# Strassen's scheme in the last group of each down projection, with the embedding's projection recorded inside it

## The chip, the cores and the metric

The kernel runs on one core of a Trainium2 chip. A core has a matrix engine (TensorE, PE in the profile, with PEld for its weight loads), a vector engine (VectorE, DVE), an activation engine (ScalarE, ACT), a general engine (GpSimd, POOL) and a queue that issues DMAs (SyncE, SP). The engines run side by side, each in its own order, and wait for one another through semaphores. Operands lie in SBUF; matmuls write to banks of PSUM. The metric is the device time of one execution in microseconds.

## What is computed

The reference is a decoder trunk of two layers over 512 tokens of width 1024, in float32. The first layer mixes tokens with two kinds of attention (latent and sliding-window), the second with forgetting attention. What follows the attention is the same in both:

```python
x = _layer_norm(DN_ALPHA * x + m, ln1_g[i], ln1_b[i])
x = _layer_norm(DN_ALPHA * x + _sq_relu_mlp(x, w_up[i], w_down[i]), ln2_g[i], ln2_b[i])
gate = jax.nn.sigmoid(x @ ple_w_gate[i] + ple_b_gate[i])
x = x + gate * (p[i] @ ple_w_proj[i])

def _sq_relu_mlp(x, w_up, w_down):
    return jnp.square(jax.nn.relu(x @ w_up)) @ w_down
```

Here m is the attention's output, w_up is 1024 x 4096, w_down 4096 x 1024, ple_w_proj 256 x 1024 (the projection of the per-layer embedding p) and ple_w_gate 1024 x 1024.

## The kernel before, in words

**Products.** Each float32 factor is split into a rounded part (hi) and the rest (lo), and a product is made of three matmuls, hi hi, hi lo and lo hi (`mm3`). So each matmul of 128 x 128 by 128 x 512 comes in threes. ACT makes the rounded part; the rest is a subtraction on DVE or POOL (`split`, `piece`, `tt` at line 488).

**The feed-forward part.** The 32 blocks of 128 hidden features are worked in 8 groups of four. `up` makes one block (24 matmuls, then relu and square on ACT). A group's share of the down projection is added to x. For groups 0 to 6 this is `down_pairs`, Strassen's scheme in Winograd's form: the 512 tokens are taken as two halves, the 1024 output columns as two halves, and the four feature blocks as two pairs, and 7 products of sums and differences take the place of 8. `forms` makes the sums of activations of a pair (A11, A12, A22, S1 to S4), each with its hi and lo. `form` makes those of the weights (11, 21, 22, T1 to T4) from four raw blocks. PRODUCTS names for each product the activation form, the PSUM bank (A, B or C, two of each, one per token block) and the quarter of the output that it is added to. The banks go on accumulating from product to product, and after each product DVE adds the bank to that quarter of x (line 1350). For the last group, `down` makes the plain product: for each of the four token blocks and each half of the columns, four feature blocks are accumulated in one bank and added to x by `add_sum`, which also gives the row sums. After each token block comes `after`, which is the second layer norm (`layer_norm`) and the transposition of the block (`to_X`).

**Behind it.** `ple_proj` loads the embedding, splits it and multiplies it with two weight pieces (8 banks of 6 matmuls, lines 1370 and on). `ple` and `gate` then multiply the normed x with the gate's eight weight pieces, 24 matmuls per token block and half, and combine.

**Weights.** `weight_pieces` lists all weights in the order of their use, in pieces of 128 x 1024, which lie in that order in DRAM. `weights` hands them out and records the loads and splits ahead of use, up to 12 of the 12 buffers "w". A piece takes two of them, a form of the scheme one. Raw data comes through 2 buffers "raw" for pieces and 6 buffers "t5" for the scheme. Activations, forms, rows and partial results share 42 buffers "u".

**Order.** Nothing is issued directly: every operation is recorded with an engine, an assumed duration and the buffers that it reads and writes. `Plan.schedule` then orders the operations of all engines by a greedy simulation: on each engine, the operation goes first whose priority (its place in the record, plus `shift`) is least among those that are ready. Buffers of one kind are given in the order of the record. A flag `port` marks operations of DVE that the plan lets run only while no operation of POOL runs, and the other way around. In the attention parts the shifts are written out (EVEN, ODD). On the chip each engine keeps the order so found.

Of the kernel before, what the change touches and what calls it, by code (L numbers as in the profile page):

```python
# [36 lines left out]
P = 128  # L37
S = 512
D = 1024
TB = 4  # L40
# [20 lines left out]
WARM = 8  # L61
SPLIT = "ddddppdpppdppdpdpppp"
SCRATCH = {"e": 8 * 32 * 384, "c": 16 * S, "x": S * D}

# [29 lines left out]
def weight_pieces():  # L94
# [8 lines left out]
    def tail(l):  # L103
        def up(js):
            for j in js:
                add(D, lambda I, j=j: _cols(I["w_up"][l], slice(j * P, j * P + P)))
        up(range(4))
        for g in range(8):
            up(range(4 * g + 4, 4 * g + 6) if g < 7 else ())
            for j in range(4):  # L110
                add(D, lambda I, fb=4 * g + j: _rows(I["w_down"][l], [fb], slice(0, D)), "s" if g < 7 else "w")
            up(range(4 * g + 6, 4 * g + 8) if g < 7 else ())
        for h in range(2):
            add(D, lambda I, h=h: _rows(I["ple_w_proj"][l], (0, 1), slice(512 * h, 512 * h + 512)))
        for h in range(2):
            for q in range(4):
                add(D, lambda I, h=h, q=q: _rows(I["ple_w_gate"][l], (2 * q, 2 * q + 1), slice(512 * h, 512 * h + 512)))
# [314 lines left out]
class Trunk:  # L432
    LOOK = 5

    def __init__(self, plan, A, out, scratch, pieces):
        self.p, self.nc, self.A, self.out = plan, plan.nc, A, out
        self.scratch = scratch
        self.dram = {k: Buf(None, None, None, k) for k in scratch}
        self.pieces, off = [], 0
        for w, _, _ in pieces:  # L440
            self.pieces.append((off, w))
            off += P * w

        self.items, i = [], 0
        while i < len(pieces):
            if pieces[i][2] == "s":
                self.items += [(f, i, p) for f in self.FORMS for p in range(2)]
                i += 4
            else:
                self.items.append(("w", i, 0))  # L450
                i += 1
        self.wi, self.wt, self.ahead, self.raws = 0, [], 0, {}
        self.turn = 0
        self.X = plan.buf("xh", (P, KD, S), R, "xh"), plan.buf("xl", (P, KD, S), R, "xl")
        self.ident = plan.buf("ident", (P, P), F, "ident")
        self.op = plan.op
# [100 lines left out]

    FORMS = ("11", "21", "T2", "T1", "T3", "22", "T4")
    FORM_POOL = {"T3", "T4", "l21", "lT1", "l22"}

    def form(self, f, i, p):
# [8 lines left out]
        def less(key, out, x, y, r, w):  # L570
            self.tt(512, key in self.FORM_POOL, out, x, y, ALU.subtract, r, w)
        if f == "T2":
            t3 = self.raws[p][2] = self.u("T3")
            less("T3", lambda: t3[:], lambda: b[:, h[1]], lambda: a[:, h[1]], [(a, 1), (b, 1)], [t3])
            less("T1", lambda: a[:, h[1]], lambda: a[:, h[1]], lambda: a[:, h[0]], [(a, 0)], [(a, 1)])
            less("T2", lambda: a[:, h[0]], lambda: b[:, h[1]], lambda: a[:, h[1]], [(a, 1), (b, 1)], [(a, 0)])
# [50 lines left out]
    def rsqrt(self, y, v, r, w, n=1, scale=0):  # L627

        t, hv = self.small("nt", n), self.small("nh", n)
        d = lambda fn, rr, ww, dur=0.07: self.dve(1, fn, rr, ww, dur=dur)  # L630
        d(lambda e: e.tensor_scalar(y().bitcast(I32), v().bitcast(I32), 1, None, ALU.arith_shift_right), r, [w])
# [205 lines left out]
    def e_bias(self):  # L837
# [12 lines left out]
        self.nsinks = self.p.buf("sm16", (P, 8), F, "nsinks")  # L850
        self.dve(8, lambda e: e.tensor_scalar(self.nsinks[:], self.sinks[:], -1.0, None, ALU.mult), [self.sinks], [self.nsinks])

# [362 lines left out]
    def layer_norm(self, x, st, g, b):  # L1215

        nm, q, v, y = (self.small(n, 4) for n in ("nm", "sq", "va", "rs"))
        c = lambda z: z[:, 0:1]
        d = lambda fn, r, w, dur=0.07: self.dve(1, fn, r, w, dur=dur)
        d(lambda e: e.tensor_scalar(c(nm), st[:, 0:1], st[:, 1:2], -1.0 / D, ALU.add, ALU.mult), [st], [nm], 0.1)  # L1220
# [44 lines left out]

    def ffn(self, x, after):

        rt = self.up_first()
        for g in range(7):
            rl = [self.up() for _ in range(2)]  # L1270
            self.down_pairs(g, rt, x)
            rl += [self.up() for _ in range(2)]
            rt = [self.forms(*rl[j:j + 2]) for j in (0, 2)] if g < 6 else rl
        self.down(rt, x, after)

# [53 lines left out]

    def down_pairs(self, g, rt, x):  # L1330

        banks, seen = {}, set()
        for f, k, (th, h) in self.PRODUCTS:
            ws = [self.weights() for _ in rt]
            for i in range(2):
# [11 lines left out]
                if g == 0 and (tb, h) not in seen:  # L1347
                    self.dve(S, lambda e, b=b, xx=xx: e.scalar_tensor_tensor(xx[:], xx[:], ALPHA, b[:], ALU.mult, ALU.add), [b], [xx])
                else:
                    self.dve(S, lambda e, b=b, xx=xx: e.tensor_tensor(xx[:], xx[:], b[:], ALU.add), [b], [xx])  # L1350
                seen.add((tb, h))

    def down(self, rl, x, after):

        rt = [self.p.buf("t5", (P, 2, 512), R, "r") for _ in rl]
        for a, r in zip(rl, rt):
            self.split(S, lambda a=a: a[:], lambda r=r: r[:, 0, :], lambda r=r: r[:, 1, :], [a], [r], psum=False)
        ws = [self.weights() for _ in range(4)]
        for tb in range(TB):
            ts, st = slice(tb * P, (tb + 1) * P), self.small("st", 4)  # L1360
            for h in range(2):
                cs = slice(512 * h, 512 * (h + 1))
                b = self.bank()
                for j in range(4):
                    r, w = rt[j], ws[j]
                    self.mm3(512, lambda b=b: b[:], (lambda r=r, ts=ts: r[:, 0, ts], lambda r=r, ts=ts: r[:, 1, ts]),
                             (lambda w=w, cs=cs: w[0][:, cs], lambda w=w, cs=cs: w[1][:, cs]), j == 0, j == 3,
                             [r] + list(w), [b])
                self.add_sum(x[tb][h], b, st, h)
            after(tb, st)  # L1370

    def ple_proj(self, l):

        ph, pl = ([self.u(n, R) for _ in range(2)] for n in ("ph", "pl"))
        for k in range(2):
            raw = self.load("u", (P, S), lambda k=k: self.A["pT"][l, k], "praw")
            self.split(S, lambda raw=raw: raw[:], lambda k=k: ph[k][:], lambda k=k: pl[k][:], [raw], [ph[k], pl[k]], psum=False)
        out = {}
        for h in range(2):
            w = self.weights()  # L1380
            for tb in range(TB):
                ts = slice(tb * P, (tb + 1) * P)
                b = self.bank()
                for k in range(2):
# [3 lines left out]
                             [ph[k], pl[k]] + list(w), [b])  # L1388
                pr = self.u("pr")
                self.act(S, lambda e, b=b, pr=pr: e.mul(pr[:], b[:], 0.5), [b], [pr], True)  # L1390
                out[h, tb] = pr
        return out

# [26 lines left out]
    def run(self):  # L1420
        A = self.A
        for l in range(2):
# [24 lines left out]

            self.ffn(x, ln2)
            pr = self.ple_proj(l)
            bg = self.row(8 + l, "bg")  # L1450
# [43 lines left out]
```

## Time and profile before

| | |
|---|---|
| median of 3 runs | 1263.97 us (1263.49 to 1265.16) |
| the profiled execution | 1265.41 us, of which the span of the profile is 1263.6 |
| clock granted to TensorE, mean | 0.995 |
| DMA | 132.83 MB, 105 GB/s in the mean |

The stages of the profile, in us from the start of the span: attention of layer 0 to about 200, its feed-forward part to about 555, the gate to about 612; attention of layer 1 to about 884, its feed-forward part to about 1203, the gate to the end at 1263.6. In the profile a row names line, engine, operation, and the tiles written and read by their names in the program, without the buffer numbers. A matmul's duration includes the time in which it overlaps the next one; the rate is read from start to start, or from the length of a stretch that is full. The busy time of a DVE operation includes time in which it was held off from SBUF.

### The profile page before, as it was taken

How to read it: one execution, taken by the hardware profiler on the slowest of the kernel's cores; microseconds unless marked ns; L12 is line 12 of the kernel's file. 1: busy time of each engine (PE TensorE's matmuls, PEld its weight loads, DVE VectorE, ACT ScalarE, POOL GpSimd, SP SyncE). 2: the span in 40 equal slices, each digit the busy share in tenths (PEclk: the TensorE clock that was granted, in tenths of full speed). 3: DMA queues.
4: the chain of work that ended last, by engine and by line, in shares of the span. 5: the costliest groups of instructions: out<-in, count | busy, mean ns of one | idle time of the engine just before them, and what ended most of it. 6: DMA issues, size and time to landing. Idle time of an engine off the chain costs nothing.

```text
span 1263.6 us, 17349 instructions
## 1 busy us (share of the span) xinstructions
PE 1233.4 (98%) x6108; PEld 1042.6 (83%) x6108; DVE 949.7 (75%) x1695; ACT 687.2 (54%) x1352; POOL 505.2 (40%) x408
## 2 busy tenths in 40 slices
PE   8988999999999999999999999899999999999998
PEld 6987888988888887888897888788888888888887
DVE  5568877899888887585543587868899878897564
ACT  5658874645444445353444697945654554445451
POOL 2545432444445444312213466331544545443120
PEclk9999999999999999999999999999999999999999
DMA  5422432233223422423232422352223332332131
GB/s 197 141 88 85 145 122 85 83 101 123 89 89 100 133 75 76 154 65 131 91 104 93 147 70 92 134 183 68 84 84 114 120 100 84 117 117 82 68 117 50
DMA packets 46791, 132.83 MB, mean 105 GB/s; under 512 B 5984, under 2 KB 8672, under 8 KB 46704
## 3 DMA queue, kind: packets, MB, share of 16 engines
q1 hardware_dynamic: 46704, 131.72, 31.6%
q8 instruction: 48, 0.79, 0.3%
q14 instruction: 39, 0.32, 0.1%
HBM read 126.03 MB, written 4.62 MB: 103 GB/s over the span
## 4 chain that ended last, share of the span: by engine, by line
PE 81%; ACT 8%; DVE 6%; issue 2%; DMA 2%; POOL 1%; SPq 0%; ACTq 0%; DVEq 0%; POOLq 0%
PE mm L512 31%; PE s L512 21%; PE t L512 16%; PE o L512 10%; ACT t L664 2%; PE t L523 2%; ACT wh L551 1%; DVE wl L488 1%; DMA raw<-in_wall_dram 1%; ACT pth L502 1%; DVE qlo L753 1%; ACT q L755 1%; ACT q L752 1%; DVE t L659 1%; POOL wl L488 0%
## 5 line engine op out<-in xcount | busy, mean ns | idle before, releaser
L488 POOL TENSOR_TENSOR wl<-raw,wh 128x1024 fp32r<-128x1024 f32 (+4 forms) x78 | 182.4, 2340 | 405.5 <-ACT wh L551 376.4
L551 ACT CAST wh<-raw 128x1024 fp32r<-128x1024 f32 (+5 forms) x150 | 152.2, 1018 | 148.0 <-DMA raw<-in_wall_dram 73.7
L488 POOL TENSOR_TENSOR wf<-raw,wf 128x512 fp32r<-128x512 f32 x84 | 122.1, 1475 | 173.4 <-ACT wf L584 156.8
L512 PE MATMUL mm<-xh,wh 128*128 128x512 f32 (+1 forms) x416 | 161.7, 389 | 2.8 <-DVE k L766 0.8
L512 PE MATMUL mm<-xl,wh 128*128 128x512 f32 (+1 forms) x416 | 159.6, 384 | 0.2 <-DVE xl L503 0.2
L512 PE MATMUL mm<-xh,wl 128*128 128x512 f32 (+1 forms) x416 | 159.7, 384 | 0.0
L488 DVE TENSOR_TENSOR wl<-raw,wh 128x1024 fp32r<-128x1024 f32 (+4 forms) x72 | 102.5, 1423 | 47.8 <-ACT wh L551 38.3
L584 ACT CAST wf<-raw 128x512 fp32r<-128x512 f32 x168 | 100.9, 615 | 34.9 <-PE t L512 15.3
L512 PE MATMUL t<-wf,rh 128*128 128x512 f32 x336 | 103.8, 390 | 0.7 <-DVE x L1350 0.7
L673 POOL TENSOR_SCALAR t<-t,st 128x256 f32<-128x256 f32 (+3 forms) x128 | 69.3, 561 | 79.3 <-DVE st L670 61.4
L512 PEld LDWEIGHTS mm<-xh,wh 128*128 128x128 f32 x416 | 78.8, 189 | 19.7 <-ACT q L755 2.2
L512 PEld LDWEIGHTS mm<-xh,wl 128*128 128x128 f32 x416 | 78.7, 189 | 15.8 <-DVE wl L503 0.4
L512 PEld LDWEIGHTS mm<-xl,wh 128*128 128x128 f32 x416 | 78.7, 189 | 14.4 <-DVE xl L503 0.5
L488 DVE TENSOR_TENSOR wf<-raw,wf 128x512 fp32r<-128x512 f32 x84 | 77.4, 936 | 17.4 <-ACT wf L584 17.1
L512 PE MATMUL mm<-wh,xh 128*128 128x384 f32 (+5 forms) x232 | 82.8, 357 | 5.9 <-DVE qlo L753 2.8
L512 PE MATMUL mm<-wl,xh 128*128 128x384 f32 (+5 forms) x232 | 80.6, 348 | 0.2 <-POOL wl L488 0.2
L512 PE MATMUL mm<-wh,xl 128*128 128x384 f32 (+5 forms) x232 | 80.7, 348 | 0.0
L1350 DVE TENSOR_TENSOR x<-x,t 128x512 f32<-128x512 f32 x100 | 67.0, 679 | 12.3 <-PE t L512 10.3
L664 ACT ACTIVATE t<-t,st 128x256 f32<-128x256 f32 (+3 forms) x128 | 68.7, 540 | 12.7 <-DVE st L659 10.6
L512 PEld LDWEIGHTS t<-wf,rh 128*128 128x128 f32 x336 | 62.8, 188 | 14.7 <-DVE x L1350 1.8
L512 PE MATMUL s<-wf,rh 128*128 128x512 f32 x224 | 69.0, 389 | 0.0
L512 PE MATMUL t<-wf,rl 128*128 128x512 f32 x168 | 65.4, 389 | 0.0
(296 smaller groups left out, 3273.9 us busy)
## 6 DMA issues: line engine op xcount, KB each, us to landing
raw<-in_wall_dram SPq DMA_DIRECT2D x183, 512.0 KB, 3.5
ck<-scratch_c SPq DMA_DIRECT2D x16, 256.0 KB, 3.8
raw<-in_wall_dram SPq DMA_DIRECT2D x9, 384.0 KB, 3.3
x<-in_xT_dram SPq DMA_DIRECT2D x8, 256.0 KB, 5.3
x<-in_xn_dram SPq DMA_DIRECT2D x8, 256.0 KB, 5.3
g<-in_rows_dram SPq DMA_DIRECT2D x8, 256.0 KB, 5.1
b<-in_rows_dram SPq DMA_DIRECT2D x8, 256.0 KB, 5.3
scratch_x<-x SPq DMA_DIRECT2D x8, 256.0 KB, 2.0
```

The source lines that it names most:

```text
L488: fn = lambda e: e.tensor_tensor(out(), a(), b(), op)
L502: self.act(n, lambda e: e.copy(hi(), src()), r, w, psum)
L512: return [self.nc.tensor.matmul(o(), a(), b(), start=s, stop=e, **kw) for o, a, b, s, e in prods]
L523: lambda: [self.nc.tensor.transpose(o(), i(), self.ident[:]) for o, i in items],
L551: self.act(w, lambda e: e.copy(hi[:, :w], raw[:, :w]), [raw], [hi])
L584: self.act(512, lambda e: e.copy(t[:, h[0]], src()), [key], [(t, 0)])
L659: return e.tensor_tensor_reduce(t[:, offs[i] + a:offs[i] + z], b[:, c + a:c + z], ad(), -scale, init, ALU.add, ALU.min, nm[:, i:i + 1])
L664: self.act(n, lambda e, i=i, tt=tt: e.activation(tt(), tt(), AF.Exp, bias=nm[:, i:i + 1], scale=-1.0, accum_out=sm[:, i:i + 1]), [(nm, i)] ...
L673: self.pool(0.13 + 1.21e-3 * n, lambda e, i=i, tt=tt: e.tensor_scalar(tt(), tt(), rc[:, i:i + 1], 1.0, ALU.mult, ALU.mult), [rc], [(t, i)])
L752: self.act(S, lambda e, q2=q2, rs=rs: e.copy(q2[rs, :], bank[rs, :]), [bank], [(q2, 0)], True)
L753: self.dve(S, lambda e, q2=q2, lo=lo, rs=rs: e.tensor_tensor(lo[rs, :], bank[rs, :], q2[rs, :].bitcast(F), ALU.subtract), [bank, (q2, 0)], ...
L1350: self.dve(S, lambda e, b=b, xx=xx: e.tensor_tensor(xx[:], xx[:], b[:], ALU.add), [b], [xx])
```

## The change

1. The last group goes through `form`, `forms` and `down_pairs` like the others; `down` is removed. `down_pairs` gets two functions, `after` and `between`, for the last group alone.
2. In the last group the products are in another order (LAST): S1 before S2 and S4 before S3. So the upper half of the tokens (blocks 0 and 1) is complete after the fifth product, and the lower half (blocks 2 and 3) after the seventh. The last addition to a quarter of x is `add_sum`, and when both halves of a block are done, `after` is recorded. The last two products have their priority moved ahead by 200 places. The weight forms T1 and T2 are made in the other order there.
3. `ple_proj` is taken apart. Its loads, splits and two weight pieces are recorded before the last group (`ple_load`), its matmuls after the third product, with a priority 400 places later and the banks "o" and "s". The two pieces stand ahead of the last four down pieces in `weight_pieces`.
4. The small DVE operations of `rsqrt`, `layer_norm` and the sinks get the flag `port`.

```diff
+AHEAD = 200
+LATER = 400
...
             up(range(4 * g + 4, 4 * g + 6) if g < 7 else ())
+            for h in range(2 if g == 7 else 0):
+                add(D, lambda I, h=h: _rows(I["ple_w_proj"][l], (0, 1), slice(512 * h, 512 * h + 512)))
             for j in range(4):
-                add(D, lambda I, fb=4 * g + j: _rows(I["w_down"][l], [fb], slice(0, D)), "s" if g < 7 else "w")
+                add(D, lambda I, fb=4 * g + j: _rows(I["w_down"][l], [fb], slice(0, D)), "s" if g < 7 else "t")
...
-    FORMS = ("11", "21", "T2", "T1", "T3", "22", "T4")
+    FORMS = {"s": ("11", "21", "T2", "T1", "T3", "22", "T4"), "t": ("11", "21", "T1", "T2", "22", "T3", "T4")}
...
-        if f == "T2":
+        if f in ("T1", "T2") and t3 is None:
...
-        d = lambda fn, rr, ww, dur=0.07: self.dve(1, fn, rr, ww, dur=dur)
+        d = lambda fn, rr, ww, dur=0.07: self.dve(1, fn, rr, ww, dur=dur, port=True)
...
-        d = lambda fn, r, w, dur=0.07: self.dve(1, fn, r, w, dur=dur)
+        d = lambda fn, r, w, dur=0.07: self.dve(1, fn, r, w, dur=dur, port=True)
...
-            rt = [self.forms(*rl[j:j + 2]) for j in (0, 2)] if g < 6 else rl
-        self.down(rt, x, after)
+            rt = [self.forms(*rl[j:j + 2]) for j in (0, 2)]
+        load()
+        self.down_pairs(7, rt, x, after, between)
...
+    LAST = (*PRODUCTS[:2], PRODUCTS[3], PRODUCTS[2], PRODUCTS[5], PRODUCTS[4], PRODUCTS[6])
+
+    def down_pairs(self, g, rt, x, after=None, between=None):
 
         banks, seen = {}, set()
-        for f, k, (th, h) in self.PRODUCTS:
+        todo = self.LAST if after else self.PRODUCTS
+        sums = [self.small("st", 4) for _ in range(TB)] if after else None
+        for n, (f, k, (th, h)) in enumerate(todo):
+            if after and n == 3:
+                between()
+
+            self.p.shift = -AHEAD if after and n > 4 else 0
             ws = [self.weights() for _ in rt]
...
+                elif after and all(y != (th, h) for _, _, y in todo[n + 1:]):
+                    self.add_sum(xx, b, sums[tb], h)
...
+                if after and all(y[0] != th for _, _, y in todo[n + 1:]):
+                    shift, self.p.shift = self.p.shift, 0
+                    after(tb, sums[tb])
+                    self.p.shift = shift
+        self.p.shift = 0
...
-    def ple_proj(self, l):
+    def ple_load(self, l):
...
-        out = {}
-        for h in range(2):
-            w = self.weights()
+        return ph, pl, [self.weights() for _ in range(2)]
+
+    def ple_proj(self, ph, pl, ws):
+
+        out, shift = {}, self.p.shift
+        for h, w in enumerate(ws):
             for tb in range(TB):
                 ts = slice(tb * P, (tb + 1) * P)
-                b = self.bank()
+                b, self.p.shift = self.bank(("o", "s")[tb % 2]), LATER
```

More of the change, by code (lines that the diff above doesn't have):

```diff
@@ L109, in tail @@
             up(range(4 * g + 4, 4 * g + 6) if g < 7 else ())
+            for h in range(2 if g == 7 else 0):
+                add(D, lambda I, h=h: _rows(I["ple_w_proj"][l], (0, 1), slice(512 * h, 512 * h + 512)))
             for j in range(4):
-                add(D, lambda I, fb=4 * g + j: _rows(I["w_down"][l], [fb], slice(0, D)), "s" if g < 7 else "w")
+                add(D, lambda I, fb=4 * g + j: _rows(I["w_down"][l], [fb], slice(0, D)), "s" if g < 7 else "t")
             up(range(4 * g + 6, 4 * g + 8) if g < 7 else ())
-        for h in range(2):
-            add(D, lambda I, h=h: _rows(I["ple_w_proj"][l], (0, 1), slice(512 * h, 512 * h + 512)))
         for h in range(2):
@@ L445, in __init__ @@
         while i < len(pieces):
-            if pieces[i][2] == "s":
-                self.items += [(f, i, p) for f in self.FORMS for p in range(2)]
+            if pieces[i][2] != "w":
+                self.items += [(f, i, p) for f in self.FORMS[pieces[i][2]] for p in range(2)]
                 i += 4
@@ L850, in e_bias @@
         self.nsinks = self.p.buf("sm16", (P, 8), F, "nsinks")
-        self.dve(8, lambda e: e.tensor_scalar(self.nsinks[:], self.sinks[:], -1.0, None, ALU.mult), [self.sinks], [self.nsinks])
+        self.dve(8, lambda e: e.tensor_scalar(self.nsinks[:], self.sinks[:], -1.0, None, ALU.mult), [self.sinks], [self.nsinks], port=True)
     def e_q(self, j):
@@ L1264, in out_proj, with ffn @@
                 step(*s)
-    def ffn(self, x, after):
+    def ffn(self, x, load, between, after):
         rt = self.up_first()
@@ L1328 @@
                 ("S4", "C", (0, 1)), ("A22", "A", (1, 0)))
-    def down_pairs(self, g, rt, x):
+    LAST = (*PRODUCTS[:2], PRODUCTS[3], PRODUCTS[2], PRODUCTS[5], PRODUCTS[4], PRODUCTS[6])
+    def down_pairs(self, g, rt, x, after=None, between=None):
         banks, seen = {}, set()
-        for f, k, (th, h) in self.PRODUCTS:
+        todo = self.LAST if after else self.PRODUCTS
[4 more added lines that the diff above has]
+            self.p.shift = -AHEAD if after and n > 4 else 0
             ws = [self.weights() for _ in rt]
@@ L1351, in down_pairs @@
                 seen.add((tb, h))
[L1353 to L1362, printed above, removed]
-                b = self.bank()
[L1364 to L1370, printed above, removed]
-    def ple_proj(self, l):
+                if after and all(y[0] != th for _, _, y in todo[n + 1:]):
[4 more added lines that the diff above has]
+    def ple_load(self, l):
         ph, pl = ([self.u(n, R) for _ in range(2)] for n in ("ph", "pl"))
@@ L1377, in ple_proj @@
             self.split(S, lambda raw=raw: raw[:], lambda k=k: ph[k][:], lambda k=k: pl[k][:], [raw], [ph[k], pl[k]], psum=False)
-        out = {}
-        for h in range(2):
-            w = self.weights()
+        return ph, pl, [self.weights() for _ in range(2)]
+    def ple_proj(self, ph, pl, ws):
+        out, shift = {}, self.p.shift
+        for h, w in enumerate(ws):
             for tb in range(TB):
                 ts = slice(tb * P, (tb + 1) * P)
-                b = self.bank()
+                b, self.p.shift = self.bank(("o", "s")[tb % 2]), LATER
                 for k in range(2):
@@ L1389, in ple_proj @@
                 pr = self.u("pr")
+                self.p.shift = shift
                 self.act(S, lambda e, b=b, pr=pr: e.mul(pr[:], b[:], 0.5), [b], [pr], True)
                 out[h, tb] = pr
+        self.p.shift = shift
         return out
@@ L1446, in ln2 @@
                 self.to_X(x[tb], tb)
-            self.ffn(x, ln2)
-            pr = self.ple_proj(l)
+            pr, pw = {}, []
+            self.ffn(x, lambda: pw.extend(self.ple_load(l)), lambda: pr.update(self.ple_proj(*pw)), ln2)
             bg = self.row(8 + l, "bg")
```

## The prediction

> **What bounds the kernel now.** First the page: how busy each engine is and whose work the chain that ended last is made of.
>
> ```profile
> span 1263.6 us, 17349 instructions
> PE 1233.4 (98%) x6108; PEld 1042.6 (83%) x6108; DVE 949.7 (75%) x1695; ACT 687.2 (54%) x1352; POOL 505.2 (40%) x408
> PE 81%; ACT 8%; DVE 6%; issue 2%; DMA 2%; POOL 1%; SPq 0%; ACTq 0%; DVEq 0%; POOLq 0%
> ```
>
> TensorE (PE) works for 98% of the span and 81% of the chain. So the next view is where the missing 2% lies: the busy time by stretches. The columns are the stretch, its length, and per engine the busy time and the instructions.
>
> ```profile
> 0.00:200.00 200.00, 186.16 (x993) 159.38 (x994) 141.11 (x347) 136.56 (x321) 84.94 (x112) 0.97 0.40 128
> 200.00:235.00 35.00, 34.08 (x224) 30.88 (x223) 28.57 (x59) 19.00 (x41) 4.86 (x2) 1.00 0.28 91
> 235.00:612.00 377.00, 376.28 (x1720) 312.20 (x1718) 302.22 (x410) 184.93 (x317) 156.29 (x93) 1.00 0.30 100
> 612.00:884.00 272.00, 261.88 (x1456) 227.47 (x1455) 178.69 (x472) 167.40 (x363) 107.55 (x114) 1.00 0.34 112
> 884.00:1258.00 374.00, 374.00 (x1718) 311.87 (x1718) 297.82 (x406) 178.93 (x309) 151.60 (x88) 1.00 0.29 95
> ```
>
> The feed-forward part with the gate behind it is 235 to 612 us in layer 0 and 884 to 1258 us in layer 1. There PE is busy 376.28 of 377 and 374.00 of 374 us. Any matmul taken out there shortens the run, as long as nothing else becomes late. The attention parts hold 13.8 and 10.1 us of PE gaps.
>
> **The matmuls removed.** `down` issues 4 token blocks x 2 halves x 4 weight blocks x 3 = 96 matmuls of 512 columns in the last group of a layer. The scheme issues 7 products x 2 x 2 x 3 = 84. The busy time by stretches, once of the tile r (the last group, layer 0) and once of wf (the seventh group), and the transposes inside the first stretch from the chain in order of time:
>
> ```profile
> 530.94:555.00 24.06, 22.80 (x96) 17.74 (x95) 0.69 (x1) 0.62 (x1) 1.00 0.17 55
> 501.02:520.06 19.04, 19.04 (x84) 15.58 (x83) 1.35 (x2) 2.36 (x4) 2.56 (x2) 1.00 0.34 109
> 542.96 0.44 PE t L523 x4
> 543.40 0.44 PE s L523 x4
> 550.11 0.44 PE t L523 x4
> 550.54 0.44 PE o L523 x4
> ```
>
> The last group takes 24.06 us, of which 4 x 0.44 = 1.76 are transposes of the layer norm: 22.30 us for its 96 matmuls, 0.232 each. A group in the scheme takes 19.04 us for 84, 0.227 each. Difference 3.26 us a layer, **6.5 us in the run**. If the new group ran at the old group's 0.232, it would be 84 x 0.232 = 19.5 and 2.8 a layer; that is the other end of this term. I take 3.26, since the scheme's own group is the nearer row.
>
> The Trainium skill ("TensorE: Matmul & The Clock Gate", section "Back-to-back issue gap") gives a gap of N/2.4 + 2.5 ns, about 216 ns for 512 columns, for both kinds of group. By it twelve matmuls fewer would be an estimated 2.6 us a layer; neither row here reaches that rate.
>
> The embedding's projection (48 matmuls a layer: 2 halves x 4 blocks x 2 x 3) is moved, not changed: 48 x 0.227 = 10.9 us of PE. Its two weight pieces and its two input loads are the same DMAs; they now stand ahead of the last group's four weight pieces, which stay 512 KB each but come through the buffers of the scheme. In the stretches above DMA works for 0.17 to 0.34 of its time, so the moved issues on SP, now queued ahead of the last group's, cost nothing that I can see; on POOL one of the two pieces (2.41 us) now stands ahead of the last group's forms, and is in the count below. They hold 4 of the 12 weight buffers, leaving 8, which is four products of 2.72 us; a form therefore has some 8 us from a free buffer to its use. I cost that at zero; if that cover were gone, the price is in the next part.
>
> **What is added, beside PE.** The last group now needs the scheme's forms. A VectorE (DVE) operation whose two inputs are both in SBUF and a GpSimd (POOL) operation keep each other out, as the spread between least and greatest duration shows. Rows of the split line, 234 to 520 us: name, count, least/median/greatest ns.
>
> ```profile
> L488 DVE TENSOR_TENSOR wf<-raw,wf x42: 675/680/2387, 236.0 to 506.6; 128x512 fp32r<-128x512 f32 x42
> L488 POOL TENSOR_TENSOR wf<-raw,wf x42: 1294/1462/1837, 238.9 to 503.7; 128x512 fp32r<-128x512 f32 x42
> L488 DVE TENSOR_TENSOR s<-rl x14: 408/412/1520, 238.8 to 489.2; 128x256 f32<-128x256 f32 x14
> L488 POOL TENSOR_TENSOR raw<-raw,raw x14: 1472/1742/1750, 241.7 to 485.4; 128x512 f32<-128x512 f32 x14
> L488 POOL TENSOR_TENSOR wl<-raw,wh x14: 2392/2412/2473, 260.9 to 514.2; 128x1024 fp32r<-128x1024 f32 x14
> L488 DVE TENSOR_TENSOR wl<-raw,wh x14: 1210/1214/1766, 265.0 to 516.9; 128x1024 fp32r<-128x1024 f32 x14
> L488 POOL TENSOR_TENSOR T<-raw,raw x12: 1307/1502/1754, 250.2 to 456.6; 128x512 f32<-128x512 f32 x12
> ```
>
> I count the time of this pair, each DVE operation at its undisturbed 0.68 (512 wide), 0.41 (256) or 1.21 us (1024). Added per layer: POOL 6 x 1.46 + 2 x 1.50 + 2 x 1.74 = 15.3; DVE 12 weight operations and 6 splits of activations x 0.68 = 12.2, and 10 narrow ones x 0.41 = 4.1. Removed: four whole pieces, 2 x 2.41 + 2 x 1.21 = 7.2, and four splits x 0.68 = 2.7. Net **+21.7 us**. Against that stands the stretch from the seventh group to the old end of the projection:
>
> ```profile
> 501.00:520.06 19.06, 19.06 (x86) 15.77 (x84) 14.41 (x19) 8.49 (x13) 7.44 (x4) 1.00 0.34 108
> 520.06:531.00 10.94, 10.94 (x50) 9.06 (x49) 2.60 (x3) 4.84 (x6) 4.77 (x2) 1.00 0.43 149
> 531.00:564.00 33.00, 33.00 (x157) 27.24 (x156) 27.07 (x62) 17.68 (x38) 5.53 (x5) 1.00 0.22 72
> ```
>
> POOL has 17.7 us here, DVE 44.1. Of DVE's, some 13 adds (0.68), 8 adds with a sum (0.77) and 6 splits (0.69) read PSUM, 19 us, and about 3 us are waiting; the rest, 21, and POOL's 17.7 make 39 of 63 us. Afterwards it is 39 + 21.7 = 60.7 in 63 - 3.3 = 59.7 us. That is more than the time, but the norms of blocks 2 and 3 (8 x 0.75 us) and two gate pieces (3.6) can slide behind the first gates, which leaves 51, or 86%. The same count for a group in the middle gives 20.1 + 18 x 0.68 + 10 x 0.41 + 2 x 1.21 = 38.9 of its 40.9 us, 95%, and PE has no gaps there. So the price lies between nothing (less is excluded, as PE has no gap here to close) and, if nothing slid and 95% were the limit, 60.7/0.95 - 59.7 = 4.2 us a layer.
>
> One small stall I do expect. In the new order the products S3 and A22 follow each other on the same two PSUM banks, each bank only free when DVE has added it; behind A22 stand the transposes of block 0 and the gates. The nearest row is the one stall of this kind in the feed-forward part (timeline of PE, in brackets the idle time and its releaser):
>
> ```profile
> 478.44 0.73 PE L512 MATMUL t<-wf,rh 128*128 128x512 f32 x2 [0.72 <-DVE x L1350]
> ```
>
> I take 0.7 us a layer for all stalls of the group, **+1.4 us**: nearer to nothing than to 4.2, since the projection's 10.9 us is ready work for such gaps.
>
> The Trainium skill ("SBUF — State Buffer", section "Who interferes with whom") says that whichever of the two engines starts first holds the pair for its whole instruction. The greatest 2387 ns of an operation that needs 675 agrees. By it alone, with nothing sliding, the sum would be that rival's, below.
>
> **The flag on the small operations.** The tiny steps of the norms now count as users of that pair in the plan. It alters no instruction, but the plan is greedy, so it may order the attention parts anew. A tiny step can indeed be caught (timeline of DVE):
>
> ```profile
> 536.72 0.69 DVE L1212 CUSTOM_DVE_ANT_0 x<-s,x 128x512 f32<-128x512 f32 x1
> 544.66 0.68 DVE L503 TENSOR_TENSOR xl<-s,xh 128x512 fp32r<-128x512 f32 x1
> 553.07 0.68 DVE L1212 CUSTOM_DVE_ANT_0 x<-mm,x 128x512 f32<-128x512 f32 x1
> 554.34 2.36 DVE L1228 SCALAR_TENSOR_TENSOR va<-sq 128x1 f32<-128x1 f32 x1
> ```
>
> The step that writes va took 2.36 us here, with POOL at work, and 0.15 elsewhere. Avoiding such catches might gain the 0.9 us of PE gaps at 200 to 235 us, where layer 0's first norms run, and little more; a worse order in the attention parts might cost a quarter of their 24.0 us of gaps, 6 us. I take **+1.0**: the list of priorities there was fitted to the old costs, and a change of order is more likely to lose than to win.
>
> **The sum.** -6.5 + 1.4 + 1.0 = -4.1 us. The profiled execution took 1265.41 us (span 1263.6 and 1.8 around it); the median shown is 1263.97, which lies 1.4 below it. What lies around the span is not touched, so the difference goes on the median: **1259.9 us**.
>
> **Rivals.**
> 1. *The pair of DVE and POOL decides.* For it: 60.7 us of work for 59.7 us. Against it: what can slide, and the 95% that groups in the middle reach. With half of the 4.2 us lost in each layer: -6.5 + 4.2 + 1.0 = -1.3, about 1262.7 us; 1267 with all of it.
> 2. *Slower: the norms at the end are bare.* Before, blocks ended one by one, 6 us apart; now blocks 0 and 1 end together after S4, and 2 and 3 after A22. By the rows above, block 0 needs from its last add at 536.72 to its last split at 544.66 + 0.68 some 8.6 us until the gate may start. PE has S3 and A22, 5.4 us, for that. If the projection has been spent in earlier gaps, 3.2 us are bare, and 2.4 more where a tiny step is caught, and the 0.7 above: 6.3 us a layer, so -6.5 + 12.6 + 1.0 = +7.1, 1271 us. At least 14 of the projection's 48 matmuls kept for after S4 (14 x 0.227 = 3.2) exclude the bare part; the run turns slower from a gap of 4.0 us a layer on. Against it: little else asks for the fillers earlier. The forms of the last two activations need some 5 us after the last up product (two ACT steps, two sums, a split), and A11 and A12 give 5.4.
> 3. *The attention parts, re-ordered, lose the 6 us.* -6.5 + 1.4 + 6 = +0.9, 1264.9 us. For it: the flag touches every norm; against it: no instruction changes.
>
> **How the numbers follow.** The forecast has 0.57, with its own range 1256.5 (no stalls and 1 us won by order) to 1262 (half of rival 1). Rival 1 has 0.20, rival 2 0.13, rival 3 0.10. A measurement of this kernel can tell about 0.2%, 2.5 us, from no change, so faster is below 1261.4 and slower above 1266.5. Faster: 0.52 of the forecast, 0.04 of rival 1, 0.02 of rival 3, 0.58. Same: 0.05 + 0.14 + 0.06 = 0.25. Slower: 0.13 + 0.02 + 0.02 = 0.17. The range 1256.5 to 1268 leaves out the far end of rival 2 and a little at the bottom.
>
> **What would show it.** The last group as 84 matmuls at 0.227 us on the tile wf, with the projection's matmuls partly between them; PE without gaps over 1 us from the seventh group to the gate; 24 matmuls fewer in all. Rival 1 would show PE idle before S1, S4 or A22 with DVE or POOL splits as releaser; rival 2 PE idle before the first gate with DVE's norm as releaser; rival 3 more PE gaps before 200 us or in the odd layer's attention. A PE gap of more than 4 us in either layer's last group would make the forecast wrong.

## The result, and the profile after

The changed kernel takes 1277.7 us (median; 1275.94 to 1280.25) where the kernel before takes 1263.73: a ratio of 1.011, with an interval of 1.0094 to 1.0126. By the medians it is 14.0 us slower. The forecast was 4 us faster, and the range ended at 1268.

First the page again, busy times and the chain that ended last:

```profile
span 1276.0 us, 17421 instructions
PE 1233.7 (97%) x6084; PEld 1039.4 (81%) x6084; DVE 987.8 (77%) x1751; ACT 699.9 (55%) x1380; POOL 525.8 (41%) x424
PE 75%; ACT 8%; DVE 5%; issue 2%; DMA 1%; POOL 1%; SPq 0%; ACTq 0%; DVEq 0%; POOLq 0%
```

The 24 matmuls are gone (6084 instead of 6108), yet PE's busy time did not fall and its share of the chain went from 81% to 75%. So there are new gaps, and part of the matmuls ran slower. To find where, I compare marks that both traces have: the first matmul of the first of the eight groups and the first of the last group, in each layer. Timeline of PE, before (layer 0, layer 0, layer 1, layer 1):

```profile
254.78 2.88 PE L512 MATMUL t<-wf,a 128*128 128x512 f32 x12
530.94 0.40 PE L512 MATMUL mm<-wh,r 128*128 128x512 f32 x1
903.48 2.88 PE L512 MATMUL t<-wf,a 128*128 128x512 f32 x12
1178.25 0.40 PE L512 MATMUL mm<-wh,r 128*128 128x512 f32 x1
```

and the same places after:

```profile
260.86 2.88 PE L514 MATMUL t<-wf,a 128*128 128x512 f32 x12
535.86 2.88 PE L514 MATMUL t<-wf,a 128*128 128x512 f32 x12
912.04 2.88 PE L514 MATMUL t<-wf,a 128*128 128x512 f32 x12
1187.85 2.88 PE L514 MATMUL t<-wf,a 128*128 128x512 f32 x12
```

| stretch | before | after | difference |
|---|---|---|---|
| start to the first group, layer 0 | 254.78 | 260.86 | +6.1 |
| first to last group, layer 0 | 276.16 | 275.00 | -1.2 |
| last group of layer 0 to the first group of layer 1 | 372.54 | 376.18 | +3.6 |
| first to last group, layer 1 | 274.77 | 275.81 | +1.0 |
| last group of layer 1 to the end of the span | 85.35 | 88.15 | +2.8 |

There are two losses. One lies ahead of everything that the change was about: 6.1 us in the attention and first norms of layer 0, where no operation was changed, but only their order by the flag. The other lies in the two stretches where 3.3 us each should have been won: 6 to 7 us worse than that. These are marks of one execution each, and a mark can move by some 2 us (in run 2 below, again without the flag, the first group starts at 252.77 and not 254.78), so the runs are judged by their times first.

The second one, in layer 0. Timeline of PE, the idle time and its releaser (what it waited for) in brackets:

```profile
566.75 0.66 PE L525 MATMUL mm<-ident,x 128*128 128x128 f32 x4 [0.81 <-DVE x L1239]
570.87 0.72 PE L525 MATMUL s<-ident,x 128*128 128x128 f32 x4 [3.46 <-DVE x L1239]
```

These are the transpositions of block 0's two halves, with which the gate begins. PE has nothing else left: the last group and the projection are done, and block 0's norm is late. The busy time by stretches around it; the third figure from the end, ahead of the DMA share and GB/s, is the granted clock:

```profile
568.00:570.00 2.00, 0.00 (x0) 0.00 (x0) 1.08 (x1) 2.00 (x4) 0.91 (x1) 1.00 0.02 6
570.00:572.00 2.00, 1.13 (x6) 1.04 (x7) 2.00 (x6) 1.15 (x4) 0.00 (x0) 0.83 0.96 287
572.00:574.00 2.00, 2.00 (x7) 1.52 (x6) 2.00 (x7) 0.41 (x2) 0.00 (x0) 0.50 0.67 231
574.00:576.00 2.00, 2.00 (x9) 1.61 (x8) 2.00 (x6) 0.00 (x0) 0.00 (x0) 0.81 0.00 0
```

The two gaps, 0.81 and 3.46, make 4.27 us. The clock column (0.83, 0.50, 0.81) shows the second part of the price: after the gap the clock is halved for about 3.4 us. It cannot be seen in PE's busy time, because slow matmuls are busy too. The shortfall, 2 x (0.17 + 0.50 + 0.19), is 1.7 us; with the 4.27 us of gap that makes 6.0, nearly the whole of the 6.9 us by which this stretch missed the forecast's 3.3. In layer 1 the gaps are 0.48, 2.07 and 0.72 us, and the clock takes another 1.7 (rows in the last section): 5.0 of the 6.1 us there.

Why block 0's norm is late is read from DVE's timeline, from block 0's last addition on (551.70; the one at 553.06 is block 1's), and one row of ACT:

```profile
551.70 0.69 DVE L1214 CUSTOM_DVE_ANT_0 x<-s,x 128x512 f32<-128x512 f32 x1 [0.35 <-PE s L514]
553.06 0.69 DVE L1214 CUSTOM_DVE_ANT_0 x<-t,x 128x512 f32<-128x512 f32 x1 [0.41 <-PE t L514]
558.43 1.62 DVE L1230 SCALAR_TENSOR_TENSOR va<-sq 128x1 f32<-128x1 f32 x1
565.95 0.75 DVE L1239 SCALAR_TENSOR_TENSOR x<-x,rs,b 128x512 f32<-128x512 f32 x1
568.92 1.23 DVE L490 TENSOR_TENSOR wl<-raw,wh 128x1024 fp32r<-128x1024 f32 x1 [2.23 <-ACT wh L553]
570.07 0.75 DVE L1239 SCALAR_TENSOR_TENSOR x<-x,rs,b 128x512 f32<-128x512 f32 x1
572.38 0.68 DVE L505 TENSOR_TENSOR xl<-s,xh 128x512 fp32r<-128x512 f32 x1
```

```profile
567.84 1.05 ACT L553 CAST wh<-raw 128x1024 fp32r<-128x1024 f32 x1
```

Block 0 took from 551.70 to the end of its last split at 573.06: 21.4 us. The step va (the sum under the norm's square root, one column) took 1.62 us; undisturbed it takes 0.15. The last step of the norm's second half (570.07) stood on DVE behind the subtraction of a gate piece (568.92), which waited 2.23 us for its rounding on ACT (567.84). In the prediction this path was given 8.6 us.

### The profile page after: what moved, and what is told of

The parts are those of the page before. It is cut to its first block, busy times and chain, and to the rows that moved or that the text cites. A ratio compares the mean times of both kernels' runs of the same rounds, so it can differ in the third digit from the quotient of the medians.

```text
span 1276.0 us, 17421 instructions
## 1 busy us (share of the span) xinstructions
PE 1233.7 (97%) x6084; PEld 1039.4 (81%) x6084; DVE 987.8 (77%) x1751; ACT 699.9 (55%) x1380; POOL 525.8 (41%) x424
## 4 chain that ended last, share of the span: by engine, by line
PE 75%; ACT 8%; DVE 5%; issue 2%; DMA 1%; POOL 1%; SPq 0%; ACTq 0%; DVEq 0%; POOLq 0%
PE mm L514 26%; PE s L514 19%; PE t L514 18%; PE o L514 10%; ACT t L666 2%; PE t L525 1%; ACT wh L553 1%; ACT pth L504 1%; DVE wl L490 1%; DMA raw<-in_wall_dram 1%; DVE ptl L505 1%; DVE t L661 1%; ACT q L757 1%; DVE xl L505 1%; DVE qlo L755 0%
## 5 line engine op out<-in xcount | busy, mean ns | idle before, releaser
L490 POOL TENSOR_TENSOR wl<-raw,wh 128x1024 fp32r<-128x1024 f32 (+4 forms) x74 | 172.9, 2337 | 382.8 <-ACT wh L553 309.2
L553 ACT CAST wh<-raw 128x1024 fp32r<-128x1024 f32 (+4 forms) x142 | 144.1, 1016 | 148.2 <-DMA raw<-in_wall_dram 73.6
L490 POOL TENSOR_TENSOR wf<-raw,wf 128x512 fp32r<-128x512 f32 x96 | 140.8, 1488 | 179.5 <-ACT wf L586 159.5
L586 ACT CAST wf<-raw 128x512 fp32r<-128x512 f32 x192 | 115.6, 616 | 43.6 <-PE t L514 17.4
L490 DVE TENSOR_TENSOR wl<-raw,wh 128x1024 fp32r<-128x1024 f32 (+4 forms) x68 | 94.8, 1394 | 36.2 <-ACT wh L553 23.1
L514 PE MATMUL t<-wf,rh 128*128 128x512 f32 x384 | 118.5, 390 | 0.7 <-DVE x L1363 0.7
L490 DVE TENSOR_TENSOR wf<-raw,wf 128x512 fp32r<-128x512 f32 x96 | 88.9, 939 | 18.9 <-ACT wf L586 18.5
L514 PEld LDWEIGHTS t<-wf,rh 128*128 128x128 f32 x384 | 71.7, 188 | 16.5 <-DVE x L1363 1.6
L514 PE MATMUL s<-wf,rh 128*128 128x512 f32 x256 | 78.8, 389 | 0.0
L514 PE MATMUL t<-wf,rl 128*128 128x512 f32 x192 | 74.8, 389 | 0.0
```

Of the source, the lines that this page charges most:

```text
L490: fn = lambda e: e.tensor_tensor(out(), a(), b(), op)
L514: return [self.nc.tensor.matmul(o(), a(), b(), start=s, stop=e, **kw) for o, a, b, s, e in prods]
L553: self.act(w, lambda e: e.copy(hi[:, :w], raw[:, :w]), [raw], [hi])
L586: self.act(512, lambda e: e.copy(t[:, h[0]], src()), [key], [(t, 0)])
```

## The experiments

**1. The flag alone.** The kernel before, with `port=True` in `rsqrt`, `layer_norm` and the sinks' step, and nothing else.

```diff
-        d = lambda fn, rr, ww, dur=0.07: self.dve(1, fn, rr, ww, dur=dur)
+        d = lambda fn, rr, ww, dur=0.07: self.dve(1, fn, rr, ww, dur=dur, port=True)
...
-        d = lambda fn, r, w, dur=0.07: self.dve(1, fn, r, w, dur=dur)
+        d = lambda fn, r, w, dur=0.07: self.dve(1, fn, r, w, dur=dur, port=True)
```

> The kernel before with nothing but the flag on the small vector operations. Theory A (the flag alone makes the plan order the first attention part anew, and that order costs the 6.1 us by which the changed kernel is late at its first group): first group's A11 at about 261 us instead of 254.8, the feed-forward parts as before, about 1270 us. Theory B (the 6.1 us come from the parts moved in the tail): within 1 us of before. If the flag helps the norms behind the feed-forward part, less than 1270.

Measured: 1269.8 us, ratio 1.0057 (1.0042 to 1.0072), 6.4 us slower than the 1263.33 of the kernel before beside it. That is theory A; the first group's mark in its trace:

```profile
259.21 2.88 PE L512 MATMUL t<-wf,a 128*128 128x512 f32 x12
```

It is 4.4 us later than before, short of the 261 expected, and the whole span is 4.6 us longer (1268.2 for 1263.6), so next to nothing is lost behind the mark. The flag changes no operation, and it costs nearly half of the whole loss.

**2. The change without the flag.** The lines of run 1's diff, the other way around, in the changed kernel:

```diff
-        d = lambda fn, r, w, dur=0.07: self.dve(1, fn, r, w, dur=dur, port=True)
+        d = lambda fn, r, w, dur=0.07: self.dve(1, fn, r, w, dur=dur)
```

> The changed kernel without the flag on the small vector operations. Theory A: A11 of the first group back at about 254.8 us, and the losses in the two tails (+3.4 and +2.8 us against before) remain: about 1271 us. Theory B: A11 stays at 261 and the time near 1277. If the flag is what keeps the tails from being worse, more than 1271.

Measured: 1264.92 us, ratio 1.0014 (1.0003 to 1.0025). Less than the 1271 of theory A: by the ratios, taking the flag away wins 12 us, not 6. So the flag also acts in the tails. Layer 1's tail falls from 88.2 to 82.8 us, 2.5 less than before the change, not far from the 3.3 of the count of matmuls. Layer 0's stretch does not fall; it has one long gap. PE, then the queue of DVE, then POOL and ACT, in layer 0:

```profile
564.71 0.80 PE L514 MATMUL mm<-wh,xl 128*128 128x512 f32 x1 [4.46 <-DVE xl L505]
```

```profile
558.29 2.37 DVE L1230 SCALAR_TENSOR_TENSOR va<-sq 128x1 f32<-128x1 f32 x1
560.58 0.74 DVE L1228 SCALAR_TENSOR_TENSOR x<-x,nm,g 128x512 f32<-128x512 f32 x1
562.83 1.23 DVE L490 TENSOR_TENSOR wl<-raw,wh 128x1024 fp32r<-128x1024 f32 x1 [1.51 <-ACT wh L553]
563.97 0.68 DVE L505 TENSOR_TENSOR xl<-mm,xh 128x512 fp32r<-128x512 f32 x1
564.57 0.68 DVE L505 TENSOR_TENSOR xl<-s,xh 128x512 fp32r<-128x512 f32 x1
```

```profile
557.87 2.78 POOL L490 TENSOR_TENSOR wl<-raw,wh 128x1024 fp32r<-128x1024 f32 x1 [3.73 <-ACT wh L553]
```

```profile
560.69 0.20 ACT L1233 ACTIVATE nt<-va 128x1 f32<-128x1 f32 x1 [1.42 <-DVE va L1230]
561.74 1.06 ACT L553 CAST wh<-raw 128x1024 fp32r<-128x1024 f32 x1
```

A step of one column is held 2.37 us by a gate piece on POOL (557.87, 2.78 us). It delays nt on ACT, behind which the next piece's rounding stands (561.74), behind which on DVE that piece's subtraction stands (562.83), and behind that block 0's first split (563.97), for which PE waits. One hold goes once around three in-order queues. A hold alone is not enough: in layer 1 the same step is held 2.36 us, and PE waits for 0.20 us only.

**3. The gate's pieces in their turn.** In the change, the priority of the last two products also holds for what `weights` records there, which are the loads and splits of the gate's pieces. Here it does not:

```diff
+            ahead, self.p.shift = self.p.shift, 0
             ws = [self.weights() for _ in rt]
+            self.p.shift = ahead
```

> The changed kernel with the weight pieces of the gate recorded in their turn: the priority that the last two products have ahead no longer holds for the loads and splits recorded with them. Theory C (the gap of 4 us before the first gate comes from a gate piece's subtraction standing on VectorE ahead of block 0's last norm step, where it waits 2.2 us for its cast on ScalarE): the gap closes to under 2 us and the clock does not fall to half, so 3 to 5 us a layer less, about 1269 us. Theory D (ScalarE is simply full from 560 to 570 us, whatever the order): gap and time unchanged within 2 us.

Measured: 1273.6 us, ratio 1.0091 (1.0075 to 1.0107): 4.1 us less than the changed kernel by the medians. That is less than the 6 to 10 of theory C, but clearly more than theory D allows. The largest gap before the gate is 1.36 us, where it was 3.46, and the clock stays at 1.00 behind it. In the trace layer 1's tail falls by 3.5 us, but layer 0's stretch by only 1.5, with a new gap of 0.74 us a little later; the rest of what theory C promised there stays open.

**4. The projection recorded last.** `between()` is called after the last product instead of before the fourth.

```diff
-            if after and n == 3:
-                between()
...
         self.p.shift = 0
+        if after:
+            between()
```

> The changed kernel with the embedding's matmuls recorded after the last product, so that none of the 48 is spent before it. In the changed kernel 15 of 48 are spent before block 0 is complete. Theory E (they filled real gaps of the last group): the 3.4 us that they filled show as waits before S2 and S4 and come off the gap before the gate, no change within 1.5 us a layer. Theory F (the gap before the gate is bare because too few matmuls are left): the gap shrinks by 3 us a layer and no new wait appears, about 1270 us.

Measured: 1306.13 us, ratio 1.0342 (1.0324 to 1.036). Both theories missed. Buffers of one kind are given in the order of the record, so the projection's banks now came after those of the transpositions. PE waited for block 0 with the projection's matmuls undone:

```profile
567.01 0.90 PE L525 MATMUL mm<-ident,x 128*128 128x128 f32 x3 [7.11 <-DVE x L1239]
```

The attention of layer 1 was ordered anew as well and became slower: the stretch from the last group of layer 0 to the first group of layer 1 is 21 us longer than in the changed kernel, which the gap explains only in part. The run does not decide between E and F. The eleventh shows what the matmuls kept back are worth.

**5. The step va in another form.** Based on run 2. va is the sum of two columns and a constant; the second column becomes a per-partition scalar. No engine's order changes.

```diff
-        d(lambda e: e.scalar_tensor_tensor(c(v), q[:, 0:1], D * EPS, q[:, 1:2], ALU.add, ALU.add), [q], [v], 0.1)
+        d(lambda e: e.tensor_scalar(c(v), q[:, 0:1], q[:, 1:2], D * EPS, ALU.add, ALU.add), [q], [v], 0.1)
```

> The changed kernel without the flag, and the norm's step that writes va in a form with one tensor input from SBUF and the other as a per-partition scalar, as the step nm has it; every engine's order stays as it was. Theory G (in layer 0 the gap of 4.46 us before the gate comes from that step being held 2.4 us by a gate piece on GpSimd, and from the queues of ScalarE and VectorE that stand behind it): va at 0.15 us everywhere, the gap under 1.5 us and no fall of the clock, 4 to 6 us less than without it, about 1260 us. Theory D (the engines are full there whatever is held): no change beyond 1.5 us, about 1264.5.

Measured: 1261.29 us, ratio 0.9995 (0.9987 to 1.0004), 2.4 us less than run 2 by the ratios. The rows of the step, least/median/greatest ns, in run 2 and here, with the wide step of the norm below:

```profile
L1230 DVE SCALAR_TENSOR_TENSOR va<-sq x16: 144/154/2387, 201.2 to 1222.3; 128x1 f32<-128x1 f32 x16
```

```profile
L1230 DVE TENSOR_SCALAR va<-sq x16: 197/205/210, 201.3 to 1218.2; 128x1 f32<-128x1 f32 x16
L1228 DVE SCALAR_TENSOR_TENSOR x<-x,nm,g x32: 732/746/2768, 199.9 to 1216.2; 128x512 f32<-128x512 f32 x32
```

va is never held any more (greatest 210 ns). The Trainium skill ("SBUF — State Buffer", section "Who interferes with whom") says that a DVE instruction with two SBUF inputs contends with a GpSimd instruction that reads SBUF, and one with at most one, outside the two-port modes, does not; here the trace agrees, 2387 against 210 ns. But theory G got less than it expected: the hold moved to the next operation with two tensor inputs (greatest 2768 ns), and the gap before the gate shrank to 3.12 us only. So this run alone does not decide between G and D; the twelfth, where no norm step is held and the gap is gone, speaks for G.

**6. The gate's first four pieces subtracted on DVE alone**, based on run 2, so that POOL is quiet there:

```diff
+        last = [i for i, x in enumerate(pieces) if x[2] == "t"][3::4]
+        self.gate_pieces = {i + n for i in last for n in range(1, 5)}
...
+        if i in self.gate_pieces:
+            return False
         return SPLIT[i] == "p" if i < len(SPLIT) else i % 2 == 1
```

> The changed kernel without the flag, and with the subtractions of the gate's first four pieces of each layer all on VectorE, so that GpSimd works on none of them while the norms run. Theory G: no va is held, the gap in layer 0 closes, about 1260 us, less what 2.4 us more of VectorE work costs. Theory D: VectorE has more to do in the same stretch, the gap grows, 1266 us or more.

Measured: 1263.45 us, ratio 1.0007 (0.9998 to 1.0017), between the two theories. Layer 0 won (its gap of 4.46 us became one of 2.25), layer 1 got gaps of 0.36, 0.93 and 0.65 us that it had not had.

**7. The flag on the RMS norms alone**, in the kernel before.

```diff
-        d = lambda fn, rr, ww, dur=0.07: self.dve(1, fn, rr, ww, dur=dur)
+        d = lambda fn, rr, ww, dur=0.07: self.dve(1, fn, rr, ww, dur=dur, port=True)
```

> The kernel before with the flag on the small operations of the RMS norms (rsqrt) alone. If that norm, which runs at 58 to 90 us, starts the re-ordering of the first attention part: the whole +6.4 us of the flag, about 1269.5 us. If it is the layer norm's flag: within 1 us of before.

Measured: 1268.29 us, ratio 1.0051 (1.0036 to 1.0066). So the flag on 24 tiny operations between 57 and 90 us makes the loss of run 1, within the intervals. What it does is seen in the stretch behind them, before and in this run:

```profile
100.00:140.00 40.00, 36.25 (x205) 31.45 (x204) 34.38 (x97) 32.93 (x86) 19.45 (x31) 0.96 0.25 73
```

```profile
100.00:140.00 40.00, 33.23 (x175) 27.71 (x174) 31.08 (x71) 27.75 (x65) 18.95 (x25) 0.96 0.24 73
129.76 0.39 PE L512 MATMUL o<-pth,vsw 128*128 128x256 f32 x1 [1.98 <-DVE ots L717]
```

The work stands in another order, PE is busy 3.0 us less in these 40 us (1.9 more in the 40 before them, 1.8 less in the 60 behind them), and waits at places where it did not. The profiled execution is the fastest of this run's four, 1265.99 us, and its first group starts only 1.8 us later than before; so the trace shows the kind of loss and not its size. And the flag did only a part of its own work: one nt step of that norm was held 2.39 us here, as in the kernel before (2.40), though another, held 1.50 us before, was free.

**8. Runs 3 and 5 together**: no flag, va in the scalar form, pieces in their turn.

> As the run with va in the scalar form, and with the gate's weight pieces recorded in their turn. If pieces ahead of the norms still cost something once nothing is held (theory C by itself): 1 to 3 us less than that run. If the held step was all: the same within 1 us.

Measured: 1256.84 us, ratio 0.9966 (0.9953 to 0.9979), against 0.9995 of run 5: 3.7 us less, more than the 1 to 3 expected. This version is faster than both kernels. What is left in layer 0 is a gap of 1.56 us, and again a hold stands ahead of it, now of a wide step of block 1's norm, with block 0's split behind it:

```profile
556.17 2.75 DVE L1228 SCALAR_TENSOR_TENSOR x<-x,nm,g 128x512 f32<-128x512 f32 x1
558.84 0.68 DVE L505 TENSOR_TENSOR xl<-mm,xh 128x512 fp32r<-128x512 f32 x1
```

**9. The scalar form of va in the kernel before**, as a control.

> The kernel before with va in the scalar form alone; orders unchanged. In the kernel before, va is held up to 2.4 us too, but PE has no gap in the tails, and 0.9 us of gap at 230 us. If the gain of the run with pieces in turn belongs to the new last group: at most 1 us less than before here. If it belongs to the scalar form: 4 us less, about 1258 us.

Measured: 1261.64 us, ratio 0.9982 (0.997 to 0.9993), 2.1 us less, between the two expected; the gap at 230 us is gone. So about half of run 8's gain is the scalar form's, which has nothing to do with the last group, and about 0.16%, 2 us, belongs to the new last group. That is about the uncertainty of the two ratios; for it speaks that run 8's two stretches from the last group on are 1.2 and 2.0 us shorter in the trace than run 9's. Run 5's gain over run 2 is also no more than this, so it says little of the tails.

**10. The flag on the layer norms alone**, in the changed kernel.

```diff
-        d = lambda fn, rr, ww, dur=0.07: self.dve(1, fn, rr, ww, dur=dur, port=True)
+        d = lambda fn, rr, ww, dur=0.07: self.dve(1, fn, rr, ww, dur=dur)
...
-        self.dve(8, lambda e: e.tensor_scalar(self.nsinks[:], self.sinks[:], -1.0, None, ALU.mult), [self.sinks], [self.nsinks], port=True)
+        self.dve(8, lambda e: e.tensor_scalar(self.nsinks[:], self.sinks[:], -1.0, None, ALU.mult), [self.sinks], [self.nsinks])
```

> The changed kernel with the flag on the layer norms' small operations only, not on those of the RMS norms and the sinks. Without any flag it was 1264.9, with all 1277.7; the flag before the first group accounts for 6.4. If the other 6.4 us are the layer norm's flag in the tails: about 1271 us, and the tail of layer 1 as long as in the changed kernel (88 us from its last group's first matmul to the end, against 82.8 without a flag). If the tails are worse only because of where the first part leaves them: about 1265 us.

Measured: 1268.56 us, ratio 1.0045 (1.0029 to 1.0061), 3.9 us above run 2 by the ratios and between the two times expected. The tails are as in the changed kernel: the gap of 3.47 us in layer 0, those of 0.48, 2.08 and 0.72 us in layer 1, whose tail is 88.2 us long. So the layer norms' flag, meant to guard these steps, makes layer 1's tail 5 us longer.

**11. The projection early**, based on run 8.

```diff
-LATER = 400
+LATER = 0
```

> The fastest version so far (no flag, scalar form, pieces in turn) with the embedding's matmuls in their turn instead of 400 places later, so that most of them are spent before block 0 is complete. If the matmuls kept for the end are what covers the norms: PE idle before the gate by up to 7 us more in each layer, 1264 to 1270 us. If the norms are covered without them: the same as that version within 1.5 us, 1257.

Measured: 1276.41 us, ratio 1.0105 (1.0083 to 1.0127), 17.6 us above run 8 by the ratios and more than either case expected. Timeline of PE before the gate in layer 0 and layer 1:

```profile
566.45 0.90 PE L525 MATMUL mm<-ident,x 128*128 128x128 f32 x3 [9.14 <-DVE x L1239]
1222.28 1.11 PE L525 MATMUL mm<-ident,x 128*128 128x128 f32 x4 [8.44 <-DVE x L1239]
```

All 48 matmuls are spent before block 0 is complete, and the norms are bare. The gaps grow by 7.6 and 8.3 us: what the matmuls kept back had covered (33 of 48 in run 8, 7.5 us). Behind the gap in layer 0 the clock stands at 0.50 from 566 to 572 us as well. That is rival 2's mechanism, with all of the matmuls spent.

**12. Runs 6 and 8 together.**

> The fastest version so far (no flag, scalar form, pieces in turn) with the first four gate pieces of each layer subtracted on VectorE alone. In that version one step of block 1's norm is still held 2.75 us by a piece on GpSimd, with block 0's last split behind it, and PE has a gap of 1.56 us. If the hold is what is left: that gap closes and the time falls 1 to 3 us, about 1255. If VectorE's own load decides (2.4 us more of it a layer): gaps before the gate in both layers, 1 to 4 us more, 1258 to 1261.

Measured: 1258.57 us, ratio 0.9961 (0.995 to 0.9973): no different from run 8. No norm step is held in either layer (va 209 ns at most, the wide step 754), and PE has no gap over 0.2 us at layer 0's gate. Its marks, the last group of layer 0 and the first of layer 1:

```profile
525.88 2.88 PE L516 MATMUL t<-wf,a 128*128 128x512 f32 x12
895.00 2.88 PE L516 MATMUL t<-wf,a 128*128 128x512 f32 x12
```

That is 369.12 us, 3.4 less than the 372.54 before. Against run 9, which has the scalar form too (371.28), it is 2.2 less, so two thirds of the twelve matmuls' 3.3 are seen here. Layer 1 gives it back: its tail is 85.1 us, as before the change (85.35), with gaps of 0.28 and 0.55 us that explain only a part; the rest is open.

## Why the prediction was wrong

Two steps failed. The flag was put at +1.0 us and came to some 10. And the norms before the gate were taken to be covered, at a price of nothing, and were not: 4.3 us of gap in layer 0, 3.3 in layer 1, and 1.7 of half clock behind each. The two overlap: the gaps of layer 1 come with the layer norms' flag (run 2, without it, has 0.20 us there), that of layer 0 does not (4.46).

**The matmuls removed** (-3.26 us a layer): right. 24 matmuls are gone. In the changed kernel the last group's 84 and the 15 of the projection among them run from 535.86 to the next one of the projection, here, without a gap:

```profile
558.30 0.39 PE L514 MATMUL o<-wh,ph 128*128 128x512 f32 x1
```

That is 22.44 us for 99, 0.227 each, the rate that the term was worked out with.

**The flag** (+1.0 us, with 6 as the far end): mis-sized by more than any other term. Alone it costs 6.4 us by run 1, nearly all of it by the RMS norms' steps (run 7), and in the tails 3.9 us more by the layer norms' steps (run 10): some 10 us. The prediction saw that the plan is greedy and that the attention's priorities were fitted to the old costs, and then took a sixth of its own bound. That is rival 3, which was given 0.10. It never asked about the tails: there it treated the flag as harmless.

**The last group's stalls** (+0.7 us a layer): here the mechanism failed. PE had no wait at S1, S4 or A22 in the last group, so the pair of DVE and POOL did not bound it as rival 1 had it. One stall of 0.74 us is left, in the seventh group of layer 1; the kernel before had one of 0.72 in layer 0, so nothing was added. What came was **rival 2**, the bare norm before the gate, and it was excluded by a wrong number. It was to need all but 14 of the projection's matmuls spent early. 33 were kept, and the gate was still bare for 4.3 us. The 8.6 us for block 0's path were read off a block that had DVE and ACT nearly to itself. With two blocks ending together, gate pieces between their steps and one step held, the path took 21.4 us in the changed kernel. The prediction counted work (86% of the pair's time) where an in-order queue was the question: what stands in front of the one operation that PE will wait for. (Its count of the pair is also off by 1: 44.1 less 19 and 3 leaves 22 us of DVE, not 21. That is about one point of the 86% and changes nothing.)

**The half clock after a gap** was in no term. It adds 1.7 us to the 4.3 us gap in layer 0, and as much in layer 1. The trace of the kernel before already had it, at 66 us (last section).

**The parts together**: the flag at the RMS norms 0.51%, the flag at the layer norms 0.31%, the rest of the change 0.14%. That is 0.96% of the 1.1% measured; the difference is within the intervals. The rest of the change, 1.8 us slower by itself, where -5.1 was forecast, turned into about 2 us faster once its queue order was mended (runs 8 and 9; near the limit of the noise).

**The range** (1256.5 to 1268) did not hold. Its upper end cut off rival 2's own 1271 and did not let two rivals come at once, though nothing in the profile kept them apart.

## What to carry to other kernels

Where work is taken out ahead of a norm or another serial chain, follow the one operation that the matrix engine will wait for through every in-order queue, and name what stands in front of it; a share of busy time says nothing of that. A change in a planner's cost model is a change of the whole program's order, to be timed by itself before it is mixed with a change of the work. And where two engines hold each other off, look first for a form of the small operation that is not held: here it was worth 2 us in the kernel before without a change of the order.

## What the runs showed of the hardware

The clock falls to half after gaps shorter than I had thought to matter. In the changed kernel's layer 1 the gaps of 0.48 and 2.07 us before the gate (the second ends at 1222.49) are followed by this; the third figure from the end is again the granted clock (0.83 in the next 2 us):

```profile
1222.00:1224.00 2.00, 1.50 (x5) 1.27 (x6) 2.00 (x6) 1.27 (x4) 0.00 (x0) 0.82 0.86 277
1224.00:1226.00 2.00, 2.00 (x6) 1.52 (x6) 2.00 (x6) 0.20 (x1) 0.00 (x0) 0.50 0.64 231
```

In run 8 the gap of 1.56 us left the clock at 1.00:

```profile
560.00:562.00 2.00, 2.00 (x11) 1.63 (x10) 2.00 (x10) 0.29 (x2) 0.00 (x0) 1.00 0.46 184
```

The kernel before has a gap of 2.06 us that stands alone, with PE full ahead of it; the gap, and the stretches from it on:

```profile
66.19 0.41 PE L512 MATMUL mm<-wh,xh 128*128 128x384 f32 x1 [2.06 <-DVE kl L1060]
66.00:68.00 2.00, 1.81 (x8) 1.84 (x9) 1.97 (x12) 1.40 (x6) 1.32 (x3) 0.75 0.28 88
68.00:70.00 2.00, 2.00 (x8) 2.00 (x7) 2.00 (x5) 1.26 (x7) 2.00 (x3) 0.50 0.00 0
70.00:72.00 2.00, 2.00 (x12) 1.97 (x11) 0.62 (x3) 0.00 (x0) 1.99 (x5) 0.90 0.42 102
```

It costs 2 x (0.25 + 0.50 + 0.10) = 1.7 us. The same gap in run 10 cost nothing:

```profile
64.07 0.41 PE L514 MATMUL mm<-wh,xh 128*128 128x384 f32 x1 [2.04 <-DVE kl L1062]
64.00:66.00 2.00, 1.93 (x11) 1.96 (x12) 2.00 (x11) 1.52 (x7) 1.44 (x4) 1.00 0.10 30
66.00:68.00 2.00, 2.00 (x14) 2.00 (x13) 2.00 (x5) 1.15 (x5) 2.00 (x2) 1.00 0.00 0
```

In the fourteen traces of this case, from 25 us on, no gap of 1.00 to 1.71 us was followed by a lower clock. Of sixteen gaps of 1.98 to 2.08 us, twelve were and four were not. All longer ones were, from 2.15 us up. So at 2 us the same stretch of work can pay 1.7 us in one execution and nothing in another; what decides it is not shown here.

The Trainium skill ("TensorE: Matmul & The Clock Gate", section "What's actually happening") has the clock fall after an idle window of about 3.4 us. The 4.3 us in layer 0 agree; the gaps of about 2 us lie below it, so by these runs the care should begin at 2 us.
